# Two value-query units in the stream's buffers, one later split, one more tick ahead of the compression products, two decay differences apart

## The chip, the cores and the metric

The kernel runs on one core of a Trainium2 chip, so nothing is shared with other cores. The metric is the device time of one execution in microseconds (us), as the median of several runs. The core's engines are TensorE (PE, matmuls; PEld is its weight load), VectorE (DVE), ScalarE (ACT), GpSimd (POOL) and SyncE (SP, which here issues the weight transfers). Each executes its own instructions in order, and they wait for each other through semaphores.

## The reference

Two transformer-like blocks run one after the other over `x` of 256 tokens and 1024 channels, in fp32. The change lies where the first block ends and the mixers of the second run, so these lines matter:

```python
def first_block(...):                       # ends with
    y = jnp.einsum('bse,ed->bsd', y, w_out[l])
    x = x + rmsnorm(y, post_norm_g[l])

def second_block(...):
    a = rmsnorm_2(h, mix_norm[i])
    proj = a @ w_in[i]
    (hg_q, hg_f, hg_i, hg_g, n_q, n_kc, n_vc, n_ks, n_vs, n_kw, n_vw, n_gate) = jnp.split(proj, ...)
    o_hg = hgrn2_mixer(hg_q, hg_f, hg_i, hg_g, ...)
    o_nsa = nsa_mixer(n_q, n_kc, n_vc, n_ks, n_vs, n_kw, n_vw, n_gate, ...)
    mixed = jnp.concatenate([o_hg, o_nsa], axis=-1)
    h = h + mixed @ w_out[i]
    h = h + peer_ffn(rmsnorm_2(h, ffn_norm[i]), ...)

def hgrn2_mixer(...):                       # a gated linear recurrence in chunks of 64
    forget = lb + (1.0 - lb) * sigmoid(f_logit); log_f = log(forget); key = 1.0 - forget
    G = cumsum(log_f) in each chunk; G_ref = G at its middle; G_last = G at its end
    a = einsum(q * exp(G - G_ref), k * exp(G_ref - G)), causal
    k_in = k * exp(G_last - G); S = d * S + k_in^T v; o = a v + (q * exp(G)) S

def nsa_mixer(...):                         # three attention branches, 8 heads in 2 groups
    kc, vc = compress(k_cmp), compress(v_cmp)   # 32-token windows: (blk + pe) @ w1, gelu, @ w2
    s_c, p_c, o_c from kc, vc;  s_s, p_s, o_s from k_slc;  s_w, p_w, o_w from k_win
    o = g0 * o_c + g1 * o_s + g2 * o_w, normed
```

## The kernel before, in words

Every large product is computed from two halves of each factor: `hi`, a rounded copy of the value, and `lo`, what the rounding left. The function `three` (lines 295 to 297) issues hi by hi, hi by lo and lo by hi as three matmuls into one PSUM bank. The weights come as 512 KB "units" of 128 x 1024 values, in the order in which class `Units` lists them. SP loads a unit into one of four `raw` buffers, ACT writes its high half (line 83), DVE its low half (line 89). A unit of class "s" goes into the stream's buffers, three of each half (`his`, `los` in the trace), one of class "h" into a holding pool of seven (`hih`, `loh`), where it stays until both token tiles (tt = 0, 1 with 128 tokens each) have used it. `U.limit` caps how many units may have been split; `U.ensure` splits up to it, at the place in the program where it is called, so on ACT and DVE a split stands ahead of whatever is written behind that call.

The order of all instructions is written out by a scheduler of generators. `tick()` advances a clock by 1.3, and each task resumes when the clock has passed the number that its last `yield n` gave; what it then emits lands in the engines' streams at that place. `feat_unit` ticks every 12 matmuls of a projection. PSUM has a pool of four small banks, `sm`; a fifth bank that is asked for waits until the first has been read.

In order, the stretch in question is this. The first block's output products (`ps_out`, units `o1`), for the first tile and then for the second, with the residual's norm between them (`p1`, `yg`, `res`, then `n20`, `n21`: the sum of squares gives a scale, `n20d` and `n21d` are identity matrices with that scale, and `ps_n` is the normed, transposed `x`, split into two halves of `a` on lines 397 and 400). Then the value-query products (`ps_nq`, units `nq`, `nk`) and their norm (`nsa_norm`: `qss`, `qn`, `kn`, transposes `ps_qT`, `ps_kT`). Then the compression's projection (units `c0`, `c1`, bank `ps_c`), the value projection (`ps_nv`) and the feed: forget gate (`ps_f`), query (`ps_hq`), value (`ps_i`) and gate (`ps_g`). Under the feed run three sorts of tasks: `compress` (`cin`, products `ps_cmp`, `ps_kc`), `nsa_cmp` and `nsa_pair` (score banks `ps_ns`, row maximum `nmx`, exponentials `es`, transposes `ps_pt`, copies `eT`, products `ps_no`; `sc` and `ps_ct` for the compressed keys), and `forget_pair` with `hgrn` (running sum `G`, the decay differences `d1` and `d2`, products `ps_kt`, `ps_S`, `ps_ho`, and the normed output `ohg`). At the end the transposes `ps_mT` of `ohg` and `on` feed the output product `ps_o`.

Of the kernel before, what the change touches and what calls it, by code (L numbers as in the profile page):

```python
# [104 lines left out]
def body(ctx: ExitStack, tc: tile.TileContext, I, out):  # L105
# [3 lines left out]
    def open_pool(stack, name, bufs=1, side=None, **kw):  # L109
        return stack.enter_context(tc.tile_pool(name=name, bufs=bufs, side=side, reuse_waits="tile", **kw))  # L110
# [7 lines left out]
    def parts_tile(name):  # L118

        t = xpool.tile([P, 2 * KD * T + 32], F32R, name=name, tag="x")  # L120
        a = 32 if name == "c" else 16
        v = t[:, a:a + 2 * KD * T].rearrange("p (c a b) -> p c a b", c=2, b=T)
        return v[:, 0], v[:, 1]
# [4 lines left out]
    def po_bank(name="po"):  # L128
        return psum.tile([P, 512], F32, name=name, tag="po", bufs=2)
# [28 lines left out]
    U = Units(nc, rawp)  # L158
# [20 lines left out]
        U.add(("o1", k), I["w1_out"][k], cls="s" if n < 10 else "h")  # L179
    end1 = len(U.seq) - 6  # L180
    for u in range(4):
        U.add(("nq", u), I["w2_nq"][u], cls="h")
    for u in range(2):
        U.add(("nk", u), I["w2_nk"][u], cls="h")
    end1h = len(U.seq)
# [66 lines left out]
    def step(t):  # L252

        try:
            t[1] = now[0] + (next(t[0]) or 0)
        except StopIteration:
            tasks.remove(t)

    def tick(dt=1.3):
        now[0] += dt  # L260
        assert now[0] < 1e4
        for t in list(tasks):
            if now[0] >= t[1] - 1e-6:
                step(t)
# [19 lines left out]
    def spawn(g):  # L284

        t = [g, 0.0]
        tasks.append(t)
        step(t)
        return g
# [133 lines left out]
    h = parts_tile("h")  # L423
# [337 lines left out]
    hold_stack = rt.enter_context(ExitStack())  # L761
    hold = open_pool(hold_stack, "hold", 7, side="right")
    U.pools["h"] = (hold, 7, 2)
    U.limit = end1 + 7
    nrm = open_pool(hold_stack, "nrm2", side="right")
    pgb = nrm.tile([P, D], F32, name="post_g")
    nc.scalar.dma_start(pgb, I["post_g"].partition_broadcast(P))
# [120 lines left out]
    def after_o1(n, tt):  # L888
        if tt == 0:
            if n in (-1, 5):  # L890
                next(ch[0])
            if n == 5:
                U.pool_part = 0.0
        else:
            if n == -1:
                next(ch[1])
            else:
                if n == 3:
                    finish(ch[0])
                if n == 5:  # L900
                    next(ch[1])
                if n == 0:
                    next(ch[0])
                U.limit += 1
                U.ensure(U.limit)

    split_tokens([("o1", k) for k in O1h],
# [13 lines left out]
    def after_nqk(n, tt):  # L921
        if tt == 0:
            if n == 0:
                next(ch[1])
            if n == 5:
                finish(ch[1])
                bq.append(po_bank("ps_nq"))
                bk.append(po_bank("ps_nk"))
                spawn(nsa_norm(0))
        else:  # L930
            tick()

    qT = b2.tile([P, 4, T], F32, name="qT")
# [64 lines left out]
    def compress(ps):  # L998

        yield 1.3  # L1000
        kv2 = cm.tile([P, 2, T], F32, name="kv2", bufs=1)
        nc.scalar.activation(flat(kv2), ps, AF.Copy)
        yield 1.3
        ksh = cm.tile([P, 2, 2, T], F32, name="ksh", bufs=1)
        nc.gpsimd.memset(ksh[64:, :, :, T - 1:], 0.0)
        for g in range(2):
            nc.scalar.dma_start(ksh[0:64, :, g, :], kv2[g * 64:(g + 1) * 64, :, :])
            nc.scalar.dma_start(ksh[64:128, :, g, 0:T - 1], kv2[g * 64:(g + 1) * 64, :, 1:T])
        cin = cm.tile([P, 2 * 16 * 30 + 66], F32, name="cin", bufs=1)
        nc.gpsimd.memset(cin[:, 960:], 0.0)  # L1010
        cinv = cin[:, :960].rearrange("p (j i g n) -> p j i g n", j=2, i=16, g=2)
        yield 5.2
        pec = cols("pe").rearrange("p (a b) -> p a b", b=16)
        for j in range(2):
            for g in range(2):
                src = bass.AP(ksh.tensor, ksh[:, j, g, 0:1].offset, [list(ksh.ap[0]), [2, 16], [16, 15]])
                nc.vector.tensor_tensor(cinv[:, j, :, g, :], src, pec[:, j, :].unsqueeze(2).to_broadcast([P, 16, 15]), OP.add)
        yield 2.6
        h1T = cm.tile([64, 2, 2, 16], F32, name="h1T", bufs=1)
        nc.gpsimd.memset(h1T, 0.0)  # L1020
        yield from sm_wait(1)
        pc = sm_bank("ps_cmp", True)
        for j in range(2):
            for i in range(16):

                c0 = (j * 16 + i) * 30
                nc.tensor.matmul(pc[:64, j * 96:(j + 1) * 96], lhsT=cw1[:, j, i], rhs=cin[:, c0:c0 + 96],
                                 start=(i == 0), stop=(i == 15))
        yield 1.3
        gx = cm.tile([64, 60], F32, name="gx", bufs=1)  # L1030
        gt = cm.tile([64, 60], F32, name="gt", bufs=1)
        nc.vector.tensor_copy(gx.rearrange("p (a b) -> p a b", b=30), pc[:64, :192].rearrange("p (a b) -> p a b", b=96)[:, :, :30])
        sm_done(pc)
        nc.vector.tensor_tensor(gt, gx, gx, OP.mult)
        nc.vector.tensor_scalar(gt, gt, 0.044715, 1.0, op0=OP.mult, op1=OP.add)
        nc.vector.tensor_tensor(gt, gt, gx, OP.mult)
        nc.scalar.activation(gt, gt, AF.Tanh, scale=math.sqrt(2.0 / math.pi))
        yield 1.3
        nc.vector.tensor_scalar(gt, gt, 0.5, 0.5, op0=OP.mult, op1=OP.add)
        for j in range(2):  # L1040
            nc.vector.tensor_tensor(h1T[:, j, :, 0:15], gt[:, j * 30:(j + 1) * 30].rearrange("p (a b) -> p a b", b=15),
                                    gx[:, j * 30:(j + 1) * 30].rearrange("p (a b) -> p a b", b=15), OP.mult)
        h1r = cm.tile([64, 2, 4, 16], F32, name="h1r", bufs=1)
        nc.vector.tensor_copy(h1r, h1T[:, 1].unsqueeze(2).to_broadcast([64, 2, 4, 16]))
        nc.gpsimd.memset(vbd, 0.0)
        yield 1.3

        yield from sm_wait(2)
        pk = sm_bank("ps_kc", True)
        nc.tensor.matmul(pk[:32, 0:64], lhsT=h1T[:, 0].rearrange("p a b -> p (a b)"), rhs=cw2[:, 0], start=True, stop=True)  # L1050
        pv = sm_bank("ps_vc", True)
        nc.tensor.matmul(pv[:, 0:64], lhsT=h1r.rearrange("p a b c -> p (a b c)"), rhs=cw2[:, 1], start=True, stop=True)
        yield 1.3
        ksq = cm.tile([32, 64], F32, name="ksq", bufs=1)
        kss = tiny.tile([P, 1], F32, name="kss")[:32]
        nc.scalar.activation(ksq, pk[:32, 0:64], AF.Square, accum_out=kss)
        for g in range(2):
            nc.vector.tensor_tensor(vbd[:, 4 * g:4 * g + 4, g], pv[:, 0:64].unsqueeze(1).to_broadcast([P, 4, 64]),
                                    hb[:, 4 * g:4 * g + 4].unsqueeze(2).to_broadcast([P, 4, 64]), OP.mult)
        yield 1.3  # L1060
        krs = rsqrt_of_sum(kss, 1, 64, EPS, "kr")
        kcn = cm.tile([32, 2, 64], F32, name="kcn", bufs=1)
        for g in range(2):
            nc.vector.tensor_scalar(kcn[:, g], pk[:32, 0:64], krs, None, op0=OP.mult)
        sm_done(pk, pv)
        nc.gpsimd.memset(kcT[:, 32:], 0.0)
        yield 2.6
        yield from sm_wait(1)
        pk2 = sm_bank("ps_kcT", True)
        nc.tensor.transpose(pk2[:, 0:32], kcn.rearrange("p a b -> p (a b)"), ident[:32, :32])  # L1070
        yield 1.3
        nc.scalar.activation(kcT[:, 0:32], pk2[:, 0:32], AF.Copy, scale=col("kn", 0))
        sm_done(pk2)
        cmp_done.append(1)
# [34 lines left out]
    def forget_pair(np_, ps):  # L1109
        sl = slice(2 * np_, 2 * np_ + 2)  # L1110
        yield 1.3
        nc.scalar.activation(flat(sg[:, sl]), ps, AF.Sigmoid)
        yield 1.3
        for j in range(2):
            n = 2 * np_ + j
            nc.vector.tensor_scalar(fg[:, n], sg[:, n], omlb[:, n:n + 1], lb[:, n:n + 1], op0=OP.mult, op1=OP.add)
        if np_ == 1:
            yield 1.3
            nc.scalar.activation(sg, fg, AF.Ln)
            yield 1.3  # L1120
            nc.vector.tensor_scalar(fg, fg, -1.0, 1.0, op0=OP.mult, op1=OP.add)
            nc.vector.tensor_tensor_scan(flat(G), flat(rst), flat(sg), 0.0, OP.mult, OP.add)
            yield 2.6
            nc.vector.tensor_tensor(d1, G, G[:, :, 31:32].to_broadcast([P, 16, 64]), OP.subtract)
            nc.vector.tensor_tensor(d2, G[:, :, 63:64].to_broadcast([P, 16, 64]), G, OP.subtract)
            hg_ready["d"] = True

# [419 lines left out]
    s = region(0, 4096).rearrange("p (t a b) -> p t a b", t=2, b=P)  # L1547
# [449 lines left out]
```

## Time and profile before

| | |
|---|---|
| median of 3 runs | 1226.26 us (1226.21 to 1227.93) |
| the profiled execution | 1224.55 us, its span 1222.8 us |
| mean granted TensorE clock | 0.997 |
| PE busy | 98% of the span |
| DVE, ACT, POOL busy | 75%, 52%, 10% |
| chain that ended last, by engine | PE 83%, DVE 10%, ACT 3%, issue 2%, DMA 2% |

The span runs from the first to the last instruction of the profiled execution. An engine's busy share counts its own instructions over the whole span; it says little about one stage. The chain that ended last is followed back from the last instruction, at each step to what released it. In a timeline, several like instructions in a row stand as one row with their count (x4), and "[2.72 <- DVE n21d ...]" says how long the engine stood idle in front of them, and what released it.

### The profile page before, as it was taken

How to read it: one execution, taken by the hardware profiler on the slowest of the kernel's cores; microseconds unless marked ns; L12 is line 12 of the kernel's file. 1: busy time of each engine (PE TensorE's matmuls, PEld its weight loads, DVE VectorE, ACT ScalarE, POOL GpSimd, SP SyncE). 2: the span in 40 equal slices, each digit the busy share in tenths (PEclk: the TensorE clock that was granted, in tenths of full speed). 3: DMA queues.
4: the chain of work that ended last, by engine and by line, in shares of the span. 5: the costliest groups of instructions: out<-in, count | busy, mean ns of one | idle time of the engine just before them, and what ended most of it. 6: DMA issues, size and time to landing. Idle time of an engine off the chain costs nothing.

```text
span 1222.8 us, 22544 instructions
## 1 busy us (share of the span) xinstructions
PE 1196.2 (98%) x8805; PEld 1080.7 (88%) x8805; DVE 920.5 (75%) x1964; ACT 632.0 (52%) x953; POOL 123.5 (10%) x192
## 2 busy tenths in 40 slices
PE   8999989899999999999999999999999999999998
PEld 7979988788887899999999999998888888888887
DVE  6799886757877589987887688888878555555566
ACT  6855655545664555545555444444444444444454
POOL 3410012000000478400000000000000000000000
PEclk9999999999999999999999999999999999999999
DMA  6454337453223755665555556555555575556571
GB/s 229 157 182 163 134 125 238 145 162 128 92 87 113 236 163 180 189 205 183 158 172 157 184 178 182 181 178 171 186 175 183 185 265 189 192 196 194 191 231 64
DMA packets 59083, 211.78 MB, mean 173 GB/s; under 512 B 6560, under 2 KB 7648, under 8 KB 58592
## 3 DMA queue, kind: packets, MB, share of 16 engines
q1 hardware_dynamic: 56736, 204.60, 51.7%
q10 hardware_dynamic: 2240, 5.75, 1.4%
q8 instruction: 69, 1.13, 0.4%
q14 instruction: 38, 0.31, 0.1%
HBM read 206.65 MB, written 3.15 MB: 172 GB/s over the span
## 4 chain that ended last, share of the span: by engine, by line
PE 83%; DVE 10%; ACT 3%; issue 2%; DMA 2%; ACTq 0%; SPq 0%; DVEq 0%
PE ps_u L295 10%; PE ps_acc L295 10%; PE ps_u L296 10%; PE ps_u L297 10%; PE ps_acc L296 10%; PE ps_acc L297 10%; DVE los L89 3%; PE ps_w L1713 1%; PE ps_w L1714 1%; ACT his L83 1%; PE ps_pq L295 1%; PE ps_pq L296 1%; PE ps_pq L297 1%; PE ps_out L297 1%; PE ps_out L295 1%
## 5 line engine op out<-in xcount | busy, mean ns | idle before, releaser
L89 DVE TENSOR_TENSOR los<-raw,his 128x1024 fp32r<-128x1024 f32 (+2 forms) x351 | 407.0, 1162 | 231.2 <-ACT his L83 229.9
L83 ACT ACTIVATE his<-raw 128x1024 fp32r<-128x1024 f32 (+1 forms) x351 | 370.0, 1057 | 330.3 <-PE ps_acc L297 168.3
L295 PE MATMUL ps_u<-x,his 128*128 128x256 f32 x1024 | 287.7, 281 | 0.0
L297 PE MATMUL ps_u<-x,los 128*128 128x256 f32 x1024 | 283.2, 277 | 0.0
L296 PE MATMUL ps_u<-x,his 128*128 128x256 f32 x1024 | 283.1, 276 | 0.0
L295 PE MATMUL ps_acc<-his,c 128*128 128x512 f32 x496 | 194.4, 392 | 0.0
L296 PE MATMUL ps_acc<-los,c 128*128 128x512 f32 x496 | 193.1, 389 | 0.0
L297 PE MATMUL ps_acc<-his,c 128*128 128x512 f32 x496 | 193.1, 389 | 0.0
L296 PEld LDWEIGHTS ps_u<-x,his 128*128 128x128 f32 x1024 | 192.4, 188 | 0.0
L297 PEld LDWEIGHTS ps_u<-x,los 128*128 128x128 f32 x1024 | 192.4, 188 | 0.0
L295 PEld LDWEIGHTS ps_u<-x,his 128*128 128x128 f32 x1024 | 192.2, 188 | 0.0
L297 PEld LDWEIGHTS ps_acc<-his,c 128*128 128x128 f32 x496 | 93.1, 188 | 19.7
L296 PEld LDWEIGHTS ps_acc<-los,c 128*128 128x128 f32 x496 | 93.2, 188 | 18.9
L295 PEld LDWEIGHTS ps_acc<-his,c 128*128 128x128 f32 x496 | 93.1, 188 | 18.9
L87 POOL TENSOR_TENSOR los<-raw,his 128x256 fp32r<-128x256 f32 x96 | 74.4, 806 | 42.6 <-ACT his L83 42.5
L1753 ACT ACTIVATE R<-ps_u 128x512 f32<-128x512 f32 x38 | 22.7, 599 | 64.3 <-PE ps_u L297 64.3
L1703 DVE TENSOR_TENSOR o<-iota,i1p 128x1024 f16<-128x1024 f16 x64 | 43.8, 684 | 0.0
L1755 ACT ACTIVATE ps_u<-ps_u 128x512 f32<-128x512 f32 x26 | 15.1, 582 | 52.6 <-PE ps_u L297 52.6
L89 DVE TENSOR_TENSOR loh<-raw,hih 128x1024 fp32r<-128x1024 f32 x30 | 36.1, 1221 | 7.3 <-ACT hih L83 5.8
L1713 PE MATMUL ps_w<-o2h,o 128*128 128x52 f16 (+1 forms) x512 | 39.7, 192 | 0.0
L1714 PE MATMUL ps_w<-o2l,o 128*128 128x52 f16 (+1 forms) x512 | 39.1, 191 | 0.0
L1781 DVE TENSOR_TENSOR c<-R,c 128x1024 fp32r<-128x1024 f32 (+2 forms) x33 | 38.8, 1177 | 0.0
(578 smaller groups left out, 2289.6 us busy)
## 6 DMA issues: line engine op xcount, KB each, us to landing
raw<-u SPq DMA_DIRECT2D x128, 512.0 KB, 3.6
raw<-v SPq DMA_DIRECT2D x128, 512.0 KB, 4.2
raw<-w_out SPq DMA_DIRECT2D x24, 512.0 KB, 3.9
raw<-wq SPq DMA_DIRECT2D x16, 512.0 KB, 4.2
raw<-w_f SPq DMA_DIRECT2D x10, 512.0 KB, 4.3
raw<-w_xl SPq DMA_DIRECT2D x8, 512.0 KB, 5.8
raw<-w_v SPq DMA_DIRECT2D x8, 512.0 KB, 3.8
raw<-w_ga SPq DMA_DIRECT2D x8, 512.0 KB, 3.8
```

The source lines that it names most:

```text
L83: nc.scalar.activation(hi[:, :n], raw[:, :n], AF.Copy)
L87: nc.gpsimd.tensor_tensor(lo[:, a:b], raw[:, a:b], hi.bitcast(F32)[:, a:b], OP.subtract)
L89: nc.vector.tensor_tensor(lo[:, :c], raw[:, :c], hi.bitcast(F32)[:, :c], OP.subtract)
L295: nc.tensor.matmul(ps, lhsT=lh, rhs=rh, start=start, stop=False)
L296: nc.tensor.matmul(ps, lhsT=lh, rhs=rl, start=False, stop=False)
L297: nc.tensor.matmul(ps, lhsT=ll, rhs=rh, start=False, stop=stop)
L1703: nc.vector.tensor_tensor(rows(o1, P), i1, pairs(i1p, tsl, P), OP.is_equal)
L1713: nc.tensor.matmul(pw[:, j], lhsT=o1[:, g0 + j], rhs=oh_[:, g0 + j, :n], start=True, stop=False)
L1714: nc.tensor.matmul(pw[:, j], lhsT=o1[:, g0 + j], rhs=ol_[:, g0 + j, :n], start=False, stop=True)
L1753: nc.scalar.activation(flat(R[0][:, 2 * ip:2 * ip + 2]), ps, AF.Gelu_apprx_tanh)
L1755: nc.scalar.activation(ps, ps, AF.Gelu_apprx_tanh)
L1781: nc.vector.tensor_tensor(flat(lo), flat(src), flat(hi.bitcast(F32)), OP.subtract)
```

## The change

Six places differ. (1) The first two value-query units become class "s". (2) The cap on splits in the output products of the second tile is two higher, so that these two are counted. (3) In that phase the cap no longer runs beyond the held units, so `c0` isn't split there. (4) `c0` is split when the first tile's norm is started, and `c1` and the first value unit when two of the second tile's value-query units have been multiplied. (5) `compress` waits one more tick ahead of its products. (6) `d1` and `d2` are issued two ticks apart and not together.

```diff
     for u in range(4):
-        U.add(("nq", u), I["w2_nq"][u], cls="h")
+        U.add(("nq", u), I["w2_nq"][u], cls="s" if u < 2 else "h")
@@
     U.pools["h"] = (hold, 7, 2)
-    U.limit = end1 + 7
+    U.limit = end1 + 9
@@ after_o1
-                U.limit += 1
+                U.limit = min(U.limit + 1, end1h)
                 U.ensure(U.limit)
@@ after_nqk
                 spawn(nsa_norm(0))
+                U.limit = end1h + 1
+                U.ensure(U.limit)
         else:
+            if n in (1, 3):
+                U.limit += 1
+                U.ensure(U.limit)
             tick()
@@ compress
-        yield 2.6
+        yield 3.9
         h1T = cm.tile([64, 2, 2, 16], F32, name="h1T", bufs=1)
@@ forget_pair
             nc.vector.tensor_tensor(d1, G, G[:, :, 31:32].to_broadcast([P, 16, 64]), OP.subtract)
+            yield 2.6
             nc.vector.tensor_tensor(d2, G[:, :, 63:64].to_broadcast([P, 16, 64]), G, OP.subtract)
```

Three places show how instructions move. On DVE, around the norm of the second tile (`n21a` to `n21d`), before:

```order
L779 SCALAR_TENSOR_TENSOR res<-yg,p1z,res 128x512 x2
L89 TENSOR_TENSOR los<-raw,his 128x1024
L376 TENSOR_SCALAR n21a<-n21q 128x1
L344 TENSOR_SCALAR n21z<-n21a 128x1
L348 TENSOR_SCALAR n21t<-n21z,n21a 128x1
L340 TENSOR_SCALAR n21u<-n21t 128x1
L340 TENSOR_SCALAR n21z<-n21u,n21z 128x1
L348 TENSOR_SCALAR n21t<-n21z,n21a 128x1
L340 TENSOR_SCALAR n21z<-n21t,n21z 128x1
L384 TENSOR_SCALAR n21d<-ident,n21z 128x128
L400 SCALAR_TENSOR_TENSOR a<-ps_n,smalls,a 128x128 x8
L957 TENSOR_REDUCE qss<-qsq 128x12
```

The same place on DVE in the changed kernel, where line numbers are up to six higher:

```order
L779 SCALAR_TENSOR_TENSOR res<-yg,p1z,res 128x512 x2
L376 TENSOR_SCALAR n21a<-n21q 128x1
L344 TENSOR_SCALAR n21z<-n21a 128x1
L348 TENSOR_SCALAR n21t<-n21z,n21a 128x1
L340 TENSOR_SCALAR n21u<-n21t 128x1
L340 TENSOR_SCALAR n21z<-n21u,n21z 128x1
L348 TENSOR_SCALAR n21t<-n21z,n21a 128x1
L340 TENSOR_SCALAR n21z<-n21t,n21z 128x1
L384 TENSOR_SCALAR n21d<-ident,n21z 128x128
L400 SCALAR_TENSOR_TENSOR a<-ps_n,smalls,a 128x128 x8
L89 TENSOR_TENSOR los<-raw,his 128x1024 x2
L962 TENSOR_REDUCE qss<-qsq 128x12
```

The split of `c0` in front of `n21a` is gone, and two splits (`c0` and `c1`) stand between the low halves of `a` and `qss`.

On DVE behind the first softmax rows of the compressed keys, in front of the second score pair's maximum (`nmx`), before:

```order
L1254 RECIPROCAL cm<-cm 128x8
L1255 TENSOR_TENSOR cm<-cm,gtt 128x8
L1256 TENSOR_TENSOR sc<-sc,cm 128x128
```

```order
L1294 TENSOR_SCALAR nmx<-nmx 128x4
L1133 SCALAR_TENSOR_TENSOR qs<-th_3466,ps_hq 128x512
L1124 TENSOR_TENSOR d_3142<-G 128x1024
L1125 TENSOR_TENSOR d_3143<-G 128x1024
L89 TENSOR_TENSOR los<-raw,his 128x1024
L1290 ISA es,nmx<-ps_ns,ald 128x128
```

The same place on DVE in the changed kernel, from `d1` (d_3142) to the first maximum, and then from that maximum's end to the second pair's:

```order
L1129 TENSOR_TENSOR d_3142<-G 128x1024
L1257 TENSOR_TENSOR sc<-sc,cmask 128x128
L1258 TENSOR_REDUCE cm<-sc 128x8
L1259 TENSOR_SCALAR cm<-cm 128x8
L1260 RECIPROCAL cm<-cm 128x8
L1261 TENSOR_TENSOR cm<-cm,gtt 128x8
L1262 TENSOR_TENSOR sc<-sc,cm 128x128
L1296 ISA es,nmx<-ps_ns,ald 128x128
```

```order
L1300 TENSOR_SCALAR nmx<-nmx 128x4
L89 TENSOR_TENSOR los<-raw,his 128x1024
L1131 TENSOR_TENSOR d_3143<-G 128x1024
L1296 ISA es,nmx<-ps_ns,ald 128x128
```

`d1` now stands ahead of the six softmax rows and of the first pair's maximum; `d2` still stands ahead of the next maximum, behind a split.

On PE, from the last state products to the transposes `ps_mT` of the first tile, before and then in the changed kernel, without the twelve rows of `ps_ho`, which stand between the two pieces:

```order
L1184 MATMUL ps_S<-ig,kiT 128x128 x4
L1271 MATMUL ps_no<-vbd,scT 128x512 x2
L1338 MATMUL ps_no<-vv,eT 128x128 x16
L1184 MATMUL ps_S<-ig,kiT 128x128 x4
L1321 MATMUL ps_pt<-ident,es 128x128 x8
```

```order
L1338 MATMUL ps_no<-vv,eT 128x128 x8
L1321 MATMUL ps_pt<-ident,es 128x128 x8
L1338 MATMUL ps_no<-vv,eT 128x128 x8
L1430 MATMUL ps_mT<-ident,ohg 128x128 x4
L1430 MATMUL ps_mT<-ident,on 128x128 x4
```

```order
L1190 MATMUL ps_S<-ig,kiT 128x128 x4
L1327 MATMUL ps_pt<-ident,es 128x128 x16
L1190 MATMUL ps_S<-ig,kiT 128x128 x4
L1291 MATMUL ps_ns<-kT,qT 128x512 x2
L1277 MATMUL ps_no<-vbd,scT 128x512 x2
L1344 MATMUL ps_no<-vv,eT 128x128 x16
```

```order
L1327 MATMUL ps_pt<-ident,es 128x128 x8
L1436 MATMUL ps_mT<-ident,ohg 128x128 x4
L1436 MATMUL ps_mT<-ident,on 128x128 x4
```

The last score products `ps_ns` now stand behind the last `ps_g` too, and of the three groups that stood between `ps_ho` and `ps_mT` one is left; the two others come later, between products of `ps_o`.

## Rows read from the trace of the kernel before

**Rows 1.** The page, part 1: busy time, share of the span, instructions of each engine.

```profile
PE 1196.2 (98%) x8805; PEld 1080.7 (88%) x8805; DVE 920.5 (75%) x1964; ACT 632.0 (52%) x953; POOL 123.5 (10%) x192
```

**Rows 2.** PE's waits from 195 to 320 us: us in total, times, longest.

```profile
PE ps_n L394 <- DVE n21d L384: 2.7, 1, 2.7
PE ps_ct L1260 <- DVE nmx L1290: 2.2, 1, 2.2
PE ps_cmp L1027 <- DVE cin L1017: 1.6, 1, 1.6
...
PE ps_qT L971 <- DVE qn L962: 0.5, 1, 0.5
...
PE ps_c L297 <- DVE los L89: 0.3, 1, 0.3
```

**Rows 3.** PE's waits from 320 to 400 us, the first of four.

```profile
PE ps_no L1338 <- ACT eT L1328: 0.3, 1, 0.3
```

**Rows 4.** DVE's timeline from 225 us: start, duration, instruction [idle before].

```profile
231.95 2.35 DVE L89 TENSOR_TENSOR loh<-raw,hih 128x1024 fp32r<-128x1024 f32 x2
...
244.93 0.95 DVE L957 TENSOR_REDUCE qss<-qsq 128x12 f32<-128x768 f32 x1
...
247.77 0.76 DVE L962 TENSOR_TENSOR qn<-ps_nq,qrz 128x256 f32<-128x256 f32 x2
```

**Rows 5.** PE's timeline at the norm, the compression and the feed's 22 steps.

```profile
250.11 0.60 PE L971 MATMUL ps_qT<-ident,qn 128*128 128x128 f32 x4
...
271.22 5.00 PE L1027 MATMUL ps_cmp<-cin,cw 128*64 128x96 f32 x58 [1.64 <-DVE cin L1017]
...
298.43 0.28 PE L296 MATMUL ps_hq<-a,his 128*128 128x256 f32 x1
...
300.94 0.28 PE L297 MATMUL ps_hq<-a,los 128*128 128x256 f32 x1
```

**Rows 6.** DVE's timeline from the compressed scores to the second pair's maximum.

```profile
291.70 0.35 DVE L1243 TENSOR_TENSOR sc<-ps_cs,cd 128x64 f32<-128x64 f32 x2
...
293.55 2.28 DVE L1122 TENSOR_TENSOR_SCAN G<-rst,sg 128x1024 f32<-128x1024 f32 x1
...
303.40 0.28 DVE L1290 CUSTOM_DVE_ANT_0 es<-ps_ns,ald 128x128 f32<-128x128 f32 x1
```

**Rows 7.** Windows: length, busy us of PE, PEld, DVE, ACT, POOL; PEclk, DMA, GB/s.

```profile
241.20:244.00 2.80, 2.79 (x20) 2.65 (x21) 1.38 (x6) 2.04 (x9) 0.00 (x0) 1.00 0.04 10
...
304.30:307.50 3.20, 3.20 (x18) 3.20 (x17) 3.06 (x21) 3.12 (x11) 0.00 (x0) 0.52 0.49 166
```

**Rows 8.** ACT's timeline in the tail.

```profile
347.52 0.59 ACT L1398 ACTIVATE th<-ps_g 128x512 f32<-128x512 f32 x1
348.00 1.09 ACT L1328 ACTIVATE eT<-ps_pt 128x512 f32<-128x512 f32 x2
348.95 0.53 ACT L1299 ACTIVATE es<-es,nmx 128x256 f32<-128x256 f32 x1
...
350.92 1.06 ACT L83 ACTIVATE hih<-raw 128x1024 fp32r<-128x1024 f32 x1
```

**Rows 9.** PE's timeline in the tail.

```profile
355.40 1.16 PE L1184 MATMUL ps_S<-ig,kiT 64*128 64x128 f32 x8
356.49 1.09 PE L1321 MATMUL ps_pt<-ident,es 128*128 128x128 f32 x8
...
359.40 2.05 PE L1338 MATMUL ps_no<-vv,eT 128*128 128x128 f32 x16
```

**Rows 10.** DVE's timeline in the tail.

```profile
360.45 0.68 DVE L1218 TENSOR_REDUCE hss<-osq 128x4 f32<-128x512 f32 x1
...
363.02 1.13 DVE L1222 SCALAR_TENSOR_TENSOR ohg<-ps_ho,hrz,ig 128x128 f32<-128x128 f32 x4
...
367.69 0.69 DVE L1353 TENSOR_REDUCE nss<-osq 128x8 f32<-128x512 f32 x1
...
370.30 0.76 DVE L1356 TENSOR_TENSOR on<-ps_no,nrz 128x256 f32<-128x256 f32 x2
```

## Prediction

> **What bounds the kernel now.** I read the page first: TensorE (PE) is busy for 98% of the span [rows 1]. So the time falls only where PE stops standing idle, and rises where it is made to stand idle once more; work on VectorE (DVE) or ScalarE (ACT) that moves under cover of matmuls is worth nothing. Then I read the view of PE's waits in the stretch that the edits touch, about 200 to 400 us. Before 320 us the large ones are 2.7 us for the norm's diagonal `n21d`, 2.2 us at the transpose `ps_ct`, 1.6 us for the compression's input `cin`, and small ones for `qn` and for a low half `los` [rows 2]. Between 320 and 400 us there are four waits of 0.2 to 0.3 us, 1.0 us in all [rows 3]. What the edits can remove is thus some 8 us; what they can add is bounded only by the chains behind each wait. Behind 400 us the order of the instructions is as before, and no term comes from there. From the order of the changed kernel and the durations in the engines' timelines I replayed the stretch by hand.
>
> **Edits 1 to 4: which low halves DVE makes when.** Six splits stood on DVE between `n20d` and `n21d`; now four do, since two of value-query have moved ahead of `n20d` and the one or two of the compression's units (`c0`, `c1`) behind the norm. A pair of splits takes 2.35 us, so a step is about 1.15 us [rows 4]. One of the splits now stands before the first low half of `a`, which costs PE 1.15 us there; two fewer in front of `n21d` would bring its chain 2.3 us forward, and the later start ahead of them takes about 1.0 of that back. So the n21 transposes start 1.3 us sooner. Sum here: -1.3.
>
> The two splits of `c0` and `c1` do not vanish. They now stand between the `a` halves and `qss`, and from the start of `qss` (244.93) to the end of `qn` (247.77 + 0.76) the chain takes 3.6 us [rows 4]. `qss` followed the `a` halves at once; these now end 1.3 sooner, at 243.6, then come two splits (2.3) and about 0.4 in which the second waits for the high half that ACT makes first, so `qss` starts near 246.3 and `qn` is there near 249.9. PE reached its first `ps_qT` at 250.11 without waiting [rows 5]; it now arrives 1.3 sooner, at 248.8, and waits 1.1: a wait takes the place of the one removed. In return the wait for `los` of `c1` (0.3) goes, since that split is early now, and the one at the second `ps_qT` (0.5) [rows 2]. To there the sum is -1.3 + 1.1 - 0.3 - 0.5 = -1.0. Bounds: +0.5 (if the two splits wait for ACT 1.5 us longer) and -2.1 (if `qss` isn't held up at all).
>
> **Edit 5: one more tick ahead of the compression products.** Twelve more matmuls stand before `ps_cmp`; 22 such steps take 2.51 us, so twelve are 1.37 us [rows 5]. PE waited 1.64 us there for `cin` [rows 5], which now comes about 1.1 us sooner with its producer. PE arrives 1.0 sooner and then has 1.37 of cover, so the wait falls to about 0.2 to 0.3 and 1.4 are gained: behind it PE is 2.4 us ahead. Bounds: no gain (if `cin`'s transfers don't come forward, and the cover is lost to what PE gained) and -1.64.
>
> **Edit 6 and the transpose `ps_ct`.** Here part of the gain is given back. `ps_ct` reuses a PSUM bank whose reader is DVE's row maximum `nmx` of the second score pair. From the start of the scan of `G` (293.55) to the start of that maximum (303.40) DVE works without a pause, 9.85 us, both decay differences in it [rows 6]. In the changed order the same rows stand there, the first difference ahead of the softmax rows and the second behind the first maximum: the edit takes neither out of the way. What moves is the scan: the logarithm in front of it comes some 2.9 us sooner, 2.4 from PE and the rest since one row fewer is ahead of it. But the five rows of the compressed scores, which stood ahead of the scan (291.70 on, 1.2 us), now stand behind it [rows 6], and a split there waits about 1.3 for the high half that ACT makes behind the logarithm. So `nmx` comes 2.9 - 1.2 - 1.3 = 0.4 sooner. This bank, not PE's own arrival, sets the point: PE comes 2.4 us sooner, has twelve more matmuls (1.4 to 1.5) to do in front, and stands idle some 3 us in two pieces instead of 2.2. PE leaves at -0.4 - 1.5 = -1.9. Bounds: -1.4 (nothing sooner) and -3.2 (the split doesn't wait).
>
> Right behind it PE's granted clock falls to 0.52, which is its level of 1.2 GHz, for 3.2 us, in which about half the work is done: some 1.5 us are lost. After the 2.7 us without a matmul before 241.2 it stayed at 1.00, the level of 2.4 GHz [rows 7]. I keep the fall in the sum, since the wait in front of it isn't shorter. The Trainium skill, "TensorE: Matmul & The Clock Gate", Part 1 (The HAM clock gate), says that the throttled clock is the default, that sustained activity releases it, and that its phase differs from run to run. The traces agree in so far as one wait was followed by it and a longer one was not; by that rule any of the new waits below could be followed by half clock, and the sum would be 1.5 us more for each.
>
> **The tail, 345 to 385 us.** The scores' chains (a tick later by edit 5) and the hidden state's (two ticks later by edit 6) end against the same last matmul of the feed. What stood under feed matmuls now stands behind them, close to its producer. Four waits are new:
> - the low half of the last gate unit, 0.4 (its high half stands one place later on ACT);
> - the second bank of the last scores `ps_ns` is free only when ACT has copied `eT` of the pair before. From the end of the transposes before that, ACT does two copies (0.95), four exponentials (1.97), a tanh (0.5), a high half (1.0) and one copy (0.5): 4.9 us [rows 8]. PE does eight transposes (1.0), a state product (1.1) and half of the scores (0.3): 2.4 [rows 9]. Of the 2.5 left, 0.3 is a wait that transposes had anyway: 2.2;
> - `ps_mT` of the first token tile needs `ohg`. From the end of the last `ps_ho` (359.4) over the square and `hss` (360.45) to its first part (363.02 + 0.3) takes 3.9 us [rows 9, 10]. `ps_no`, `ps_pt` and `ps_no` covered it from 359.40 on (2.05, 1.0 and 2.05); now a single `ps_pt` group does (1.0), with 0.2 of switching: 2.7;
> - `ps_mT` of the second tile needs `on`, whose sum `nss` now stands behind `ohg` on DVE. From `ps_ho` over `ohg` 6.1 us (3.9, three more parts at 0.3, and 1.3 for splits ahead of `hss`), then `nss` to the end of `on`, 367.69 to 371.06, 3.4 [rows 10]: 9.5. PE has 24 output matmuls and eight value products in that time, 8.2: 1.3.
> Together 6.6, less the 1.0 that the tail waited before, less 0.4 since the first wait lets ACT and DVE catch up for those behind it: +5.2. Bounds: 0.4 for the tail (all four but the first covered, none of the 1.0 gone) and 6.6.
>
> **Sum.** -1.9 + 5.2 = +3.3 us. The profiled execution took 1224.55 us, 1.7 less than the median 1226.26 of the three runs; the replay is a difference, so I put it on the median: 1229.6.
>
> **The rivals.**
> - *Forecast*: the late waits come as replayed, +1 to +6, so 1227.3 to 1232.3. For it: the order is fixed and the durations are rows. Against it: each new wait is the difference of two long chains. Chance 0.55.
> - *The late waits are half covered*: ACT and DVE reach the tail as early as PE did, and half of the 6.6 stays: -1.9 + 3.3 - 1.0 = +0.4, 1226.7. For it: ACT is idle between its groups in the tail of before. Against it: the four exponentials stand in one block ahead of the copies. Chance 0.22.
> - *Faster, the other side*: one mechanism at `ps_ct`. If ACT's high half is there in time, `nmx` comes 1.7 sooner, the wait there is under the 2.2 of before and the clock doesn't fall: PE leaves at -3.2 - 1.5 = -4.7. With the tail half covered (+2.3) that is -2.4, with it wholly covered -4.7: 1221.6 to 1223.9. It decides from where the idle piece at `ps_ct` is too short for the clock to fall, and needs some cover in the tail (with none it ends at +0.5). For it: the three gains ahead of `ps_ct` are simple. Against it: ACT has a logarithm and an exponential of another table in that place. Chance 0.13.
> - *More half clock*: PE's clock falls behind one or two of the tail's waits of 2 us or more, as it did behind the 2.2 us at `ps_ct`, at 1.5 us each: +1.5 to +3 on the forecast, 1231.1 to 1232.6. For and against it: of two such waits before, one was followed by it. Chance 0.10. This is the case of the page of the Trainium skill named above.
>
> **How the numbers follow.** The time is the forecast's centre, 1229.6. The range runs from 1224.0, where the faster case ends, to 1232.6; some 0.12 lies below and 0.07 above. 0.2% is 2.45 us, about what a measurement of this kernel can tell from no change: under 1223.8 is faster, over 1228.7 slower. Of the forecast's 0.55 some 0.38 lie above 1228.7 and the rest within; the clock case is slower (0.10); of the covered case 0.17 are the same, 0.03 slower, 0.02 faster; of the faster case 0.10 are faster and 0.03 the same. That is 0.12 faster, 0.37 same, 0.51 slower; I move 0.03 from same to faster, since the step at `ps_ct` is the replay's least sure.
>
> **What would show each step.** In PE's waits of the changed kernel: `n21d` shorter by more than 1 us and the first low half `a` about 1.5; a new wait of about 1 us for `qn` at the first `ps_qT`; `cin` under 0.6; `ps_ct` still for `nmx`, with half clock behind it; and behind the last `ps_g` waits of 1 us or more at `ps_ns` for `eT` and at `ps_mT` for `ohg` and for `on`. The prediction is wrong if the clock stays up at `ps_ct`, if the tail's waits sum to under 3 us, or if the clock falls anywhere else.

## The result, and the profile after

The changed kernel takes 1232.41 us (median, 1229.03 to 1235.38) against 1225.59 us for the kernel before in the runs beside it: the ratio is 1.0055, 95% interval 1.0043 to 1.0067, so it is 6.8 us slower. Forecast were 3.3 us more, 1229.6, with a range to 1232.6.

The view of PE's waits in the changed kernel, as [rows 2, 3] for the one before, first from 195 to 320 us and then from 320 to 410 us (us in total, times, longest):

```profile
PE ps_ct L1266 <- DVE nmx L1296: 2.3, 1, 2.3
PE ps_nq L297 <- DVE a L400: 1.5, 1, 1.5
PE ps_qT L976 <- DVE qn L967: 1.4, 1, 1.4
PE ps_n L394 <- DVE n20d L384: 0.7, 1, 0.7
PE ps_ns L1291 <- DVE nmx L1296: 0.6, 1, 0.6
PE ps_n L394 <- DVE n21d L384: 0.3, 1, 0.3
```

```profile
PE ps_mT L1436 <- DVE ohg L1228: 2.6, 1, 2.6
PE ps_ns L1291 <- ACT eT L1334: 2.2, 1, 2.2
PE ps_mT L1436 <- DVE on L1362: 1.7, 1, 1.7
...
PE ps_g L296 <- DVE los L89: 0.3, 1, 0.3
```

The waits for `n21d` and `cin` are nearly or wholly gone, those for `a` and `qn` have come, `ps_ct` waits as before (with a new piece of 0.6 us for `nmx` at `ps_ns` ahead of it), and behind the last `ps_g` stand the three waits that were foreseen. What was not in the sum is in the view of windows over the tail (length, busy us of PE, PEld, DVE, ACT, POOL, then PEclk, the granted clock):

```profile
345.00:350.00 5.00, 2.82 (x6) 1.07 (x6) 3.07 (x4) 4.67 (x8) 0.00 (x0) 0.94 0.52 140
350.00:355.00 5.00, 5.00 (x30) 4.31 (x29) 4.90 (x22) 0.00 (x0) 0.00 (x0) 0.72 0.51 172
355.00:360.00 5.00, 3.53 (x38) 3.00 (x36) 2.01 (x8) 2.46 (x9) 0.00 (x0) 1.00 0.34 105
360.00:365.00 5.00, 3.82 (x16) 2.98 (x17) 4.15 (x19) 4.27 (x14) 0.00 (x0) 0.80 0.00 0
365.00:370.00 5.00, 5.00 (x31) 4.33 (x30) 2.40 (x7) 0.85 (x1) 0.00 (x0) 0.85 0.31 90
```

A mean of 0.72 over five microseconds is a stretch at 0.50, the level of 1.2 GHz, and the rest at 1.00. Missing clock times length: (0.06 + 0.28) x 5 = 1.7 us behind the wait for `eT`, (0.20 + 0.15) x 5 = 1.75 us behind the wait for `ohg`. In the kernel before the clock was 1.00 in the whole tail.

The mean granted clock of each execution is on record too, in steps of 0.001 (1.2 us of the span). (1 - clock) x span, averaged over the executions of a kernel, is an estimate of what half clock costs it anywhere in the span; below it is called the clock loss. It is 6.7 us in the changed kernel (10 executions) and 3.4 in the kernel before (64, beside the experiments). So of the 6.8 us some 3.3 are the clock, and some 3.5 are left for the waits.

Executions differ by some microseconds ahead of this stretch already: the first `n20d` transpose starts at 226.0 us in the profile of before and at 223.6 in that of after. So the two traces are compared from that transpose on, at points that both have (us since it, from PE's timelines; at `ps_cmp` and `ps_ct` the changed kernel has done twelve more matmuls, 1.4 us of work, which its column counts as gained):

| | before | after | gained | forecast |
|---|---|---|---|---|
| first transpose with `n21d` | 15.2 | 13.9 | 1.3 | 1.3 |
| second `ps_qT` | 34.2 | 33.2 | 1.0 | 1.0 |
| `ps_cmp` | 45.2 | 43.3 | 1.9 + 1.4 = 3.3 | 2.4 |
| `ps_ct` | 78.0 | 76.9 | 1.1 + 1.4 = 2.5 | 1.9 |
| first `n3d` transpose, behind the tail | 163.2 | 169.8 | -6.6 | -3.3 |

The last row of the table agrees with the 6.8 us of the medians. Between `ps_ct` and `n3d` 9.1 us are lost, where 5.2 had been worked out.

### The profile page after: what moved, and what is told of

It reads as the page before. It is cut to its first block, busy times and chain, and to the rows that moved or that the text cites. A ratio compares the mean times of both kernels' runs of the same rounds, so it can differ in the third digit from the quotient of the medians.

```text
span 1227.3 us, 22544 instructions
## 1 busy us (share of the span) xinstructions
PE 1196.8 (98%) x8805; PEld 1080.5 (88%) x8805; DVE 922.3 (75%) x1964; ACT 631.7 (51%) x953; POOL 123.1 (10%) x192
## 4 chain that ended last, share of the span: by engine, by line
PE 78%; DVE 12%; ACT 5%; issue 2%; DMA 1%; POOL 1%; ACTq 0%; SPq 0%; DVEq 0%; POOLq 0%
PE ps_u L295 10%; PE ps_acc L295 10%; PE ps_u L296 9%; PE ps_u L297 9%; PE ps_acc L296 9%; PE ps_acc L297 9%; DVE los L89 3%; ACT his L83 2%; PE ps_w L1719 1%; PE ps_w L1720 1%; PE ps_pq L296 1%; PE ps_pq L297 1%; PE ps_pq L295 1%; PE ps_out L295 1%; PE ps_out L297 1%
## 5 line engine op out<-in xcount | busy, mean ns | idle before, releaser
L89 DVE TENSOR_TENSOR los<-raw,his 128x1024 fp32r<-128x1024 f32 (+1 forms) x353 | 409.5, 1162 | 228.5 <-ACT his L83 226.3
L83 ACT ACTIVATE his<-raw 128x1024 fp32r<-128x1024 f32 x353 | 372.3, 1057 | 325.2 <-PE ps_acc L297 168.3
L89 DVE TENSOR_TENSOR loh<-raw,hih 128x1024 fp32r<-128x1024 f32 x28 | 33.5, 1220 | 8.4 <-ACT hih L83 8.3
```

What stands on the lines that cost most here:

```text
L83: nc.scalar.activation(hi[:, :n], raw[:, :n], AF.Copy)
L89: nc.vector.tensor_tensor(lo[:, :c], raw[:, :c], hi.bitcast(F32)[:, :c], OP.subtract)
```

## Experiments

Each kernel ran beside the kernel before, in five rounds. The three factors are edits 1 to 4 (splits), edit 5 (a tick ahead of the compression products) and edit 6 (the decay differences).

**Edits 1 to 4 alone.** The kernel before with the four edits of `U.add`, `U.limit`, `after_o1` and `after_nqk`.

> The kernel before with edits 1 to 4 alone (the value-query units' class and the places of the splits). Theory: the front gains about 1.0 us up to the second ps_qT (n21d's wait nearly gone, a new wait of 1.1 to 1.4 for qn at the first ps_qT), the wait for cin stays at about 1.6, and the tail has the waits of the kernel before (1 us in all, none at ps_ns): 0 to 2 us faster than before, ratio 0.998 to 1.000. Rival: the splits' new places are what made the whole change slow, through the new wait for qn: 2 us or more slower, ratio 1.002 or more.

Measured 1223.65 against 1225.63 us, ratio 0.9975 (0.9960 to 0.9991): 2.0 us faster, at the edge of what the theory had. The rival falls: the new wait for `qn` is there (1.4 us) and the whole still gains. In the profiled execution the wait for `cin` was 2.1 us, and half clock followed it, which it did not before. That execution is not the rule: its mean clock, 0.997, is among the lowest of the twelve (up to 1.000), and their clock loss is 1.7 us, against 3.3 in the kernel before beside it.

**Edit 5 alone.**

```diff
-        yield 2.6
+        yield 3.9
         h1T = cm.tile([64, 2, 2, 16], F32, name="h1T", bufs=1)
```

> The kernel before with edit 5 alone (the compression products one tick later). Theory: the later tick alone moves the last scores behind the last gate matmul and makes the tail's waits at ps_ns for eT (about 2.2), at ps_mT for ohg (about 2.6) and for on (1.3 to 1.7), each of the two long ones followed by about 3.2 us of half clock; with 1.4 gained at ps_cmp it is 5 to 8 us slower than before, ratio 1.004 to 1.0065. Rival: the decay differences make the waits of the hidden state (ohg), so that without edit 6 the wait at ps_mT for ohg is under 1 us and the whole is at most 3 us slower.

Measured 1237.02 us, ratio 1.0091 (1.0067 to 1.0115): 11.4 us slower, more than either theory gave it. Its waits of PE from 320 us on show the tail of the changed kernel complete, without edit 6:

```profile
PE ps_mT L1430 <- DVE ohg L1222: 2.6, 1, 2.6
PE ps_ns L1285 <- ACT eT L1328: 2.2, 1, 2.2
PE ps_mT L1430 <- DVE on L1356: 1.6, 1, 1.6
```

So the delay of `ohg` does not come from the decay differences. Beyond the tail it waits 1.7 us for `nmx` at `ps_ns` and 1.1 at `ps_ct`, where before had 2.2 in all, and its clock is at half for longer in the tail, from 351 to 357 us and from 368 to 371. It is at half around the transpose `ps_ct` too, from 303 to 307 us, as before had it there.

**Everything but edit 5.**

> The changed kernel without edit 5 (edits 1 to 4 and 6). Theory: the tail is that of the kernel before, no wait over 0.5 us from ps_ns to ps_mT and no half clock there; 0 to 2 us faster than before, ratio 0.998 to 1.000. Rival (edit 6 delays the hidden state): ohg's wait at ps_mT is over 1 us still, 2 us or more slower than before.

Measured 1221.70 us, ratio 0.9960 (0.9945 to 0.9976): 3.9 us faster than before, more than expected, since edit 6 gains at `ps_ct`. Its wait there, from the view of PE's waits:

```profile
PE ps_ct L1266 <- DVE nmx L1296: 1.1, 1, 1.1
```

and its order on DVE (timeline), then that of the changed kernel at the same place:

```profile
298.22 0.28 DVE L1296 CUSTOM_DVE_ANT_0 es<-ps_ns,ald 128x128 f32<-128x128 f32 x1
...
299.25 1.22 DVE L1131 TENSOR_TENSOR d<-G 128x1024 f32<-128x1024 f32 x1
```

```profile
298.73 1.22 DVE L1131 TENSOR_TENSOR d<-G 128x1024 f32<-128x1024 f32 x1
299.86 0.28 DVE L1296 CUSTOM_DVE_ANT_0 es<-ps_ns,ald 128x128 f32<-128x128 f32 x1
```

Without edit 5 (first fence) `d2` falls behind the second pair's maximum, the wait at `ps_ct` is 1.1 us and the granted clock, 1.000 in the mean of the execution, doesn't fall (over the twelve executions the clock loss is 0.5 us, against 1.7 with edits 1 to 4 alone). With edit 5 (second fence) the scores are a tick later, the maximum too, and `d2` is ahead of it again.

**Edit 5 with the tick taken back later.** The changed kernel, and

```diff
         nc.gpsimd.memset(kcT[:, 32:], 0.0)
-        yield 2.6
+        yield 1.3
         yield from sm_wait(1)
```

> The changed kernel with one tick less ahead of the transpose of kcn, so that the scores start at the tick at which they started before, while the compression products keep their later tick. Theory: the order of the tail is that of the kernel before, so its waits and the two stretches of half clock are gone, and what the front gained (2 to 2.6 us up to ps_ct) is kept, less a wait of up to 1 us for kcn: 1 to 3 us faster than before, ratio 0.9975 to 0.999. Rival (the tail's waits come from PE being ahead of ACT and DVE, not from the order): waits of over 3 us in all stay in the tail, and it is slower than before.

Measured 1221.50 us, ratio 0.9961 (0.9947 to 0.9975): 4.1 us faster than before. With the compression products where edit 5 put them and the scores where they were, the tail's waits and the half clock are gone. From 320 us to the last `ps_mT` the longest waits are those of before, 0.3 and 0.2:

```profile
PE ps_no L1344 <- ACT eT L1334: 0.3, 1, 0.3
PE ps_pt L1327 <- DVE nmx L1296: 0.3, 1, 0.3
...
PE ps_mT L1436 <- DVE ohg L1228: 0.2, 1, 0.2
```

**The reverse: only the scores a tick later.** Everything but edit 5, and

```diff
         nc.gpsimd.memset(kcT[:, 32:], 0.0)
-        yield 2.6
+        yield 3.9
         yield from sm_wait(1)
```

> The changed kernel with the compression products at their old tick, and the later tick put ahead of the transpose of kcn instead. Theory: it is the tick at which the scores start that makes the tail, not the place of the compression products; the waits at ps_ns for eT (about 2.2) and at ps_mT for ohg (2.6) and on (1.6) are there again, with two stretches of half clock: 1230 to 1235 us, ratio 1.004 to 1.008. Rival: the products' place matters (a bank that they hold longer); then the tail's waits are under 2 us in all and it is near the 1221.7 us of the kernel without edit 5.

Measured 1234.31 us, ratio 1.0058 (1.0045 to 1.0072), 12.6 us slower than the same kernel with that tick at 2.6 (0.98% by the two ratios), and in ratio as slow as the changed kernel. The waits for `eT`, `ohg` and `on` are back at 2.2, 2.6 and 1.7. So the place of the compression products costs nothing that these runs can tell, and the tick at which the scores start costs all of it.

**Edit 6 alone.**

> The kernel before with edit 6 alone (the decay differences two ticks apart). Theory: as between the run with edits 1 to 4 alone and the one with edits 1 to 4 and 6 (1223.65 and 1221.70 us), the wait at ps_ct falls from 2.2 to about 1.1 us and the half clock behind it is gone; the tail stays that of the kernel before: 1 to 3.5 us faster than before. Rival: the gain needs the earlier front of edits 1 to 4; then ps_ct still waits about 2 us and the time is within 1 us of before.

Measured 1225.75 against 1226.73 us, ratio 0.9985 (0.9974 to 0.9997): in the profile the wait at `ps_ct` is 1.1 us and its half clock is gone, as the theory had it, but the gain of 1.0 us is at the lower end, between the two. The profiled execution has the highest mean clock of the twelve, 0.999. Over all of them the clock loss is 2.55 us, against 2.95 in the kernel before beside it, so over all of them hardly any half clock is gone; where the others have theirs their record does not tell. In the profile the wait for `n21d` is still 2.7 and that for `cin` 1.7.

**Everything but edit 6.**

> The changed kernel without edit 6 (edits 1 to 5). Theory: with the scores a tick later, ps_ct waits over 2 us with or without edit 6 and the tail is the same, so it is within 2 us of the changed kernel, 1230.5 to 1234.5. Rival: edit 6 gains at ps_ct here too, as without edit 5; then it is 2 us or more slower than the changed kernel, over 1234.5.

Measured 1233.79 us, ratio 1.0055 (1.0041 to 1.0068), the ratio of the changed kernel: under edit 5 the decay differences make no difference. Here `ps_ns` waits 1.7 and `ps_ct` 1.1 for `nmx`; in the changed kernel it was 0.6 and 2.3, the same sum within 0.1.

**Work for PE in the waits.** The changed kernel with matmuls whose results nobody reads, ahead of the last scores and of the first `ps_mT`; nothing of the computation is left out:

```diff
+    def filler(bank, n):
+        for _ in range(n):
+            nc.tensor.matmul(bank[:, 384:512], lhsT=ident, rhs=ident, start=True, stop=True)
...
         pss = [sm_bank("ps_ns", True), sm_bank("ps_ns", True)]
+        if (qb, j) == (1, 3):
+            filler(pss[0], 18)
...
         pt = sm_bank("ps_mT")
+        if (kp, tt) == (0, 0):
+            filler(pt, 22)
```

> The changed kernel with idle work for PE in the tail's two long waits: 18 matmuls of 128 x 128 into the bank of the last scores before these, and 22 into the bank of the first transposes before these (their results are overwritten or never read; nothing of the computation is left out). Theory: the waits themselves (2.2 and 2.6) are filled, the time at which eT and ohg come stays, and since PE isn't idle its clock stays at 1.00 through the tail: two stretches of 3.2 us at half clock go, 2.5 to 3.5 us faster than the changed kernel's 1232.4, so 1229 to 1230. Rival: the clock falls for another reason, and the time is that of the changed kernel or up to 1 us longer.

Measured 1232.03 us, ratio 1.0038 (1.0024 to 1.0052). This alone decides nothing, since the filling was twice too long. Each of these fp32 matmuls shows as two records, so 18 of them take 4.29 us against a wait of 2.2, and 22 take 5.08 us against 2.6:

```profile
348.28 4.29 PE L788 MATMUL ps_ns<-ident 128*128 128x128 f32 x36
...
361.86 5.08 PE L788 MATMUL ps_mT<-ident 128*128 128x128 f32 x44
```

PE did some 4.6 us more than the waits held and the time stayed that of the changed kernel, which speaks for a saving of about that size; the clock was 1.00 from 309 to 420 us. So it was run again with half the number, 9 and 11, beside the changed kernel.

> The changed kernel with half as many idle matmuls in the tail's two waits as in the run before it (9 and 11; each is executed as two passes of 0.12 us, so 2.1 and 2.5 us against waits of 2.2 and 2.6). Nothing of the computation is left out. Theory: eT and ohg come when they came, no time is added, and the clock stays at 1.00 through the tail: 2.5 to 4 us faster than the changed kernel on the same chip. Rival: the time lost there is the waits' alone, and the clock's level costs nothing that they don't hide; then it is within 1 us of the changed kernel.

> The changed kernel as it is, beside the two others on the same chip: 1231 to 1234 us, ratio 1.0045 to 1.0065.

Measured 1227.85 us with the filling (ratio 1.0019, 1.0003 to 1.0035) and 1233.11 without (1.0053, 1.0032 to 1.0074): 5.3 us by the medians (0.34%, 4.2 us, by the two ratios), more than the 2.5 to 4 expected. The windows of the two traces say why. First the filled kernel's tail, then four windows of the changed kernel's in this run:

```profile
349.00:355.00 6.00, 6.00 (x37) 4.29 (x37) 5.84 (x20) 2.18 (x3) 0.00 (x0) 1.00 0.56 171
355.00:365.00 10.00, 9.80 (x84) 8.69 (x83) 7.79 (x33) 6.88 (x21) 0.00 (x0) 1.00 0.20 56
365.00:370.00 5.00, 5.00 (x31) 4.01 (x30) 3.98 (x11) 0.70 (x1) 0.00 (x0) 1.00 0.31 108
```

```profile
349.00:352.00 3.00, 2.73 (x3) 1.00 (x4) 2.90 (x4) 2.60 (x4) 0.00 (x0) 0.50 0.32 66
352.00:355.00 3.00, 3.00 (x5) 1.16 (x4) 2.93 (x15) 0.00 (x0) 0.00 (x0) 0.50 0.78 247
355.00:356.00 1.00, 1.00 (x9) 1.00 (x8) 0.98 (x6) 0.00 (x0) 0.00 (x0) 0.78 0.29 115
...
366.00:369.00 3.00, 3.00 (x10) 2.42 (x10) 2.93 (x15) 3.00 (x7) 0.00 (x0) 0.50 0.00 0
```

The waits' length is as before (`eT` and `ohg` come when they came, PE waits 0.2 us for `ohg` behind the filling), but the clock is 1.00 all through. In the unfilled run the first stretch at half clock is twice as long as in the first profile of this kernel: 1.5 + 1.5 + 0.2 us lost there and 1.5 in the last window, 4.7 together, and 5.1 with the edges of the stretches outside these windows, which is nearly the 5.3 between the medians. From `n20d` to `n3d` the filled kernel took 166.7 us, the unfilled 171.5. The other executions say the same: the clock loss is 1.7 us with the filling (12 executions) and 6.5 without (7), 4.8 us apart. So nearly the whole gain of the filling is the clock.

**The splits of `c0` and `c1` behind the first norm chain.** The kernel with the tick taken back (1221.50 us), and

```diff
                 spawn(nsa_norm(0))
-                U.limit = end1h + 1
-                U.ensure(U.limit)
         else:
-            if n in (1, 3):
+            if n in (2, 3, 5):
                 U.limit += 1
                 U.ensure(U.limit)
```

> The changed kernel with the scores' tick put back as in the run with one tick less ahead of kcn, and with the splits of c0 and c1 behind the chain of the first qn instead of ahead of it. Theory: the wait for qn at the first ps_qT (1.4 us) is gone, c0 and c1 are in time, and the front gains 1 to 1.4 us more: 1219 to 1221 us, ratio 0.995 to 0.996. Rival: c0's low half comes too late for ps_c, or the lead is lost at cin or at ps_ct, which other engines set; then it is within 0.7 us of 1221.6.

Measured 1217.59 us, ratio 0.9937 (0.9916 to 0.9958), the fastest of all: 8.4 us below the kernel before beside it. Both transposes of `qn` find it ready, as the timeline shows by the bracket that is missing:

```profile
247.61 0.60 PE L974 MATMUL ps_qT<-ident,qn 128*128 128x128 f32 x4
...
256.51 0.60 PE L974 MATMUL ps_qT<-ident,qn 128*128 128x128 f32 x4
```

From `n20d` to `n3d` it takes 157.1 us, against 158.6 with the tick taken back alone, 160.0 without edit 5, 163.2 before. The 1.5 us are the wait that is gone. The medians differ by more (3.9 us, 0.24% by the two ratios, whose intervals overlap); how much of that holds was not tried.

## Why the prediction was right, and where it was wrong

- **Edits 1 to 4**: right. `n21d` 1.3 us sooner, the wait for `a` 1.5, the new wait for `qn` 1.4 (1.1 forecast; the two splits waited 0.3 and 0.5 us for ACT's high halves), second `ps_qT` 1.0 ahead. The table shows it. The run with these edits alone gains 2.6 us between the means of all executions; 1.6 of that are clock loss, which the sum did not have, and the 1.0 that is left fits it.
- **Edit 5, its gain**: the direction was right. PE does not wait for `cin` at all, and is 3.3 us ahead at `ps_cmp` and not 2.4, partly because the wait of 0.5 for the first `los` of the feed went too. But the medians do not show the gain by itself: with the scores' tick put back, the kernels with and without the later products have the same median (1221.50 and 1221.70), though the profiled stretches differ by 1.4 us.
- **Edit 6 and `ps_ct`**: right for the whole change (some 3 us in two pieces were forecast, 0.6 and 2.3 for `nmx` came, with half clock behind them; PE leaves 2.5 ahead and not 1.9), but not as a property of edit 6. I wrote that the edit takes neither difference out of the way. Without edit 5 it does: `d2` lands behind the maximum. The rival on the other side had the outcome, the wait under 2.2 us and a clock that stays up, but from another cause (ACT's high half in time for the split, with `d2` still ahead of the maximum). The kernel without edit 5 gets that outcome because `d2` moved, and edit 5 undoes it.
- **The tail's waits**: right in place and size: 0.3, 2.2, 2.6 and 1.7 us, together 6.8 against 6.6. The step that names their cause was wrong in half: "the hidden state's (two ticks later by edit 6)". The hidden state is not later by edit 6; with edit 6 alone, or without edit 5, the tail's waits are those of before, and edit 5 alone, or a later tick at `kcn`, makes all of it. The scores' products, a tick later, no longer stand between `ps_ho` and `ps_mT`, and so they no longer cover the chain to `ohg`.
- **The clock in the tail**: this is the term that the sum lacked. I had the fall behind one wait in two, as the trace of before had it, and kept new falls out of the sum as a rival of 0.10. Two came, 1.7 and 1.75 us in the first profile and 5.1 together in the second, and filling the waits with idle matmuls took them away and gave 5.3 us. The waits (6.8 less the 1.0 of before) and the clock (3.45) make 9.25, against the 9.1 of the table; less the front's gain of 2.5 that is its 6.6. The Trainium skill, "TensorE: Matmul & The Clock Gate", Part 1 (The HAM clock gate), says that sustained activity releases the throttle and that its phase differs from run to run. Both agree here: in the filled run PE was busy through the tail and the clock stayed at 1.00, and the unfilled kernel had a fall behind `ps_ct` in one profile and none in the other.
- **The range, and the signs**: the sum of the waits, +3.3, is about what the waits cost (some 3.5), but the time that came is that of the rival with more half clock (1231.1 to 1232.6), which had a chance of 0.10. The median lies within the range by 0.2 us only, and that of the repeated run, 1233.11, lies outside: that the range held is in part luck. One of the prediction's own signs of being wrong, "if the clock falls anywhere else", came true in the first profile, and another, a clock that stays up at `ps_ct`, in the second.

Edit 5 alone loses 11.4 us, where 5 to 8 were expected. In its profile the stretch from `n20d` to `n3d` is 11.0 us longer than before (174.2 against 163.2). Half clock makes 5.1 of that (6.8 us lost, 3.4 of them behind the wait for `eT`, against 1.7 in all before), and the waits make the rest. Over its six executions the clock loss is 8.2 us, against 3.3 beside it, so this profile is no exception. What stays open is which waits the clock falls behind, and for how long. In the five profiles that have the tail's waits unfilled, half clock followed the 2.2 us for `eT` five times, with 1.7 or 3.4 us lost, and the 2.6 us for `ohg` four times; the 2.7 us for `n21d` it followed in none of three.

## What to carry to other kernels

A tick that is moved is paid for not where it stands but where its chain ends: look for what stood as cover behind the last wide work, and whether it now stands elsewhere. Where PE is to wait for 2 us or more, reckon with half clock behind the wait: here it cost 1.7 or 3.4 us more behind some of these waits, and nothing behind others. If such a wait can't be removed, idle matmuls that fill it without outlasting it can be cheaper than nothing. A profile is one execution, and its clock may be the best or the worst of all, so compare the mean granted clock of every execution before a gain is put down to the clock. When several edits touch one order, run them apart: here four of them gain 2 us, a fifth alone loses more than the whole change, and a sixth gains only without the fifth.

## What the runs showed that I had not expected

- Filling waits of 2.2 and 2.6 us with matmuls that do nothing made the kernel 5.3 us faster (1233.11 to 1227.85), though it adds work to the engine that is busy for 98% of the span.
- The clock's stretches at half differ between executions of one kernel: 3.4 us behind the wait for `eT` in one profile, 6.8 us in another, and one behind `ps_ct` in only one of them. Each 3.4 us at half lose 1.7, so two profiles of one kernel can differ by that for this alone.
